# The last quarter of `w_down` in seven half-size products, with the sums leaving PSUM through ScalarE and adding transfers

## The chip, the core and the metric

The kernel runs on one core of one Trainium2 chip. The metric is the device time of one execution in microseconds (us). Before the change it is 1189.9 us, the median of three runs (1189.68 to 1191.11).

In what follows PE is the matrix engine (TensorE), DVE is VectorE, ACT is ScalarE, POOL is GpSimd and SP is the engine that issues most transfers (DMAs). SBUF is the on-chip memory that all of them work on, PSUM the small one that PE writes its sums to.

## What is computed

A trunk of two layers over 512 frames of 1024 features. Each layer is a mixer (two attention groups of eight heads, whose outputs meet in one projection) and a squared-ReLU MLP, each behind an RMS norm and added onto the residual stream. A last norm closes the trunk. The change is in the MLP, and in the first steps of both layers.

```python
def squared_relu_mlp(h, w_up, w_down):
    return jnp.square(jax.nn.relu(h @ w_up)) @ w_down

def reference(x, positions, norm_mix, norm_mlp, norm_final, w_in_ab, ...):
    for layer in range(DEPTH):                      # DEPTH = 2
        h = rmsnorm(x, norm_mix[layer])
        if layer % 2 == 0:
            x = x + even_mixer(h, w_in_ab[e], b_forget[e], rel_bias[e], w_out_ab[e])
        else:
            x = x + odd_mixer(h, positions, w_in_cd[o], ...)
        x = x + squared_relu_mlp(rmsnorm(x, norm_mlp[layer]), w_up[layer], w_down[layer])
    return rmsnorm(x, norm_final)
```

`w_up` is 1024 x 4096 and `w_down` 4096 x 1024 per layer. All of it is float32.

## The kernel before

**Numbers.** A float32 operand is split into a high part (rounded to the format that PE takes at full rate) and a low part, the difference. A product is three matmuls: high by high, high by low, low by high (`mm3`). ACT makes each high part (a cast), DVE each low part (a subtraction). The residual stream is four tiles `X[0]` to `X[3]`, each of 128 frames by 1024 features.

**Order.** Nothing is issued while the program is written. Every operation is recorded with a priority, and `Plan` then sorts all of them into one order per engine, by its own costs for each operation and by the rotation of the buffers. That order is fixed in the program: an engine that waits for one operation holds back everything behind it in its own queue. Almost all instructions carry the line of `Plan.issue` (L230), so groups are told apart by the names of their tiles.

**MLP.** The hidden layer's 32 chunks of 128 rows are four groups of eight. `up_pair` makes two chunks with 48 matmuls of 512 columns into the PSUM tiles `mm`; DVE applies the ReLU and the norm's factor (`ex`), ACT squares (`sq`). For groups 0 to 2, `seven_products` multiplies the group's 512 x 1024 activations by the 1024 x 1024 piece of `w_down`: both are cut into 2 x 2 blocks, and with sums and differences of blocks (`into`, on DVE) seven block products do the work of eight (Winograd's form of Strassen's scheme). One block product has 24 matmuls of 512 columns into two PSUM banks. The banks `main` (tiles `pa`) run on from one product to the next, `second` and `third` (tiles `pb`) are two other pairs. After each product `add` adds its two banks onto a half of two tiles of X: 14 DVE instructions in a group. The squares are four tiles of two chunks by 512 frames, and the first product of a group waits for all four.

Numbered as the code writes them, the products are: 1 into `main`, to X's rows 0 and left half; 2 into `second`, rows 1, right; 3 and 4 into `main`, rows 1, left and right; 5 into `second`, rows 1, left; 6 into `third`, rows 0, left; 7 into `main`, rows 0, right. Rows 0 are the tiles X[0] and X[1], rows 1 are X[2] and X[3]. Between products stand the `up_pair` calls of the next group, two matmul tiles of `mm` each.

Group 3 is done plainly: `up_split` squares and splits the activations, and two `add_proj` calls multiply them by the last eight chunks of `w_down`, 4 tiles of frames x 2 halves x 8 chunks x 3 = 192 matmuls of 512 columns. The second of them (`last=True`) finishes X[0] and X[1] first and the right halves last.

**Buffers.** Weight pages (`wh`, `wl`) share eight buffers of 1024 floats per partition, the raw `w_up` blocks (`wr`) two, the raw `w_down` blocks (`rw`) nine, the pages of split activations (`sh`, `sl`) six under the name `hd`. The tiles `p3`, 128 x 512, are two.

**Start.** `load_x` loads the four tiles of X; between them `first_loads` fetches the norm's gain, copied to 128 partitions by the transfer (512 KB), and the identity, and `first_weights` three blocks of `w_in_ab`. `norm_T` normalizes each tile and turns it to feature-major form `hT`. Sixty small matmuls on zeros (`warm`) run ahead of it, twelve more (`keep_warm`) after the first tile.

**Layer 1's values** (`step`, kind "v") are two blocks of 256 columns, so 2 x 4 x 8 x 3 = 192 matmuls of 256 columns; their weights are loaded ahead of `add_proj` at the end of layer 0.

Of the kernel before, what the change touches and what calls it, by code (L numbers as in the profile page):

```python
# [17 lines left out]
P = 128  # L18
# [8 lines left out]
WARM2 = 12  # L27
# [357 lines left out]
def trunk(ctx, tc, x, positions, norm_mix, norm_mlp, norm_final, w_in_ab, b_forget, rel_bias,  # L385
# [57 lines left out]
    def load_w(view, parts=None, place="w", raw_place="w"):  # L443
# [3 lines left out]
        if raw_place == "hd":  # L447
            raw = hp.tile([P, 1024], F32, tag="hd", name=nm("wr"))
        else:
            raw = wp.tile([P, 1024], F32, tag="wr", name=nm("wr"), bufs=2)  # L450
        if place == "hd":
# [71 lines left out]
    def norm_rows(xt, g, n):  # L523

        junk = otile()
        ss = small(1)
        nc.scalar.activation(junk.bitcast(BF16)[:, :n], xt, AF.Square, accum_out=ss)
        r = rstd_of(ss, n)
        pieces = []
        for c in range(0, n, S):  # L530
            m = min(S, n - c)
            t = etile()
            nc.vector.scalar_tensor_tensor(t[:, :m], xt[:, c:c + m], r, g[:, c:c + m], ALU.mult, ALU.mult)
            pieces.append(t)
        return pieces
# [19 lines left out]

    def norm_T_(X, g_row, g=None, after=None):

        g = gain(g_row, D) if g is None else g
        hT = [(utile(), utile()) for _ in range(NC // 2)]
        for t in range(NT):  # L560
            for h, piece in enumerate(norm_rows(X[t], g, D)):
                to_feature_major(piece, 4, hT[2 * h:2 * h + 2], t)
            if t == 0 and after is not None:
                after(hT)
# [48 lines left out]
    def col_blocks(w, kc, col, n, places=None, raw_place="w"):  # L613
# [6 lines left out]
        for k, place in places:  # L620
            b = load_w(rows(w, c, c + k, col, col + n), place=place, raw_place=raw_place)
# [194 lines left out]
    def seven_products(X, R, wd, k0):  # L816
# [15 lines left out]
        a11, a21, a12, a22 = ([R[j + i][:, :, q:q + 256] for i in range(2)] for j in (0, 2) for q in (0, 256))  # L832
# [14 lines left out]
        def product(banks, A, B, first):  # L847

            for i in range(4):
                for q in range(2):  # L850
                    a = tuple(h[:, i, q * P:(q + 1) * P] for h in A)
                    b = tuple(h[:, i % 2] for h in B[i // 2])
                    mm3(banks[q], a, b, first and i == 0, i == 3, skip_group_check=not first)
# [19 lines left out]
        yield  # L873

# [11 lines left out]

        into(b11, b21, b11, SUB)
        product(second, acts(a22), weights(b11), False)
        add(second, 1, 0)
        yield  # L890

        third = side()
        product(third, acts(a12), weights(b21), True)
        add(third, 0, 0)
        yield

        into(a21, a12, a21, SUB)
        product(main, acts(a21), weights(b22), False)
        add(main, 0, 1)
        yield  # L900

    def mlp(X, g_row, wu, wd, ahead=None):
# [36 lines left out]
        def squares():  # L939
            return [up.tile([P, 2, S], F32, tag="u", name=nm("sq")) for _ in range(4)]  # L940
# [4 lines left out]
        for g in range(3):  # L945
            steps = seven_products(X, R, wd, 8 * g)
            nxt = squares() if g < 2 else None
            act = []
            for pr, n in enumerate((2, 2, 2, 1)):
# [9 lines left out]
        nxt = up_split(3584)  # L959
# [21 lines left out]
    def first_loads():  # L981
        g0.append(gain(norm_mix[0:1, :], D))
        nc.sync.dma_start(ident, consts[:, O_ID:O_ID + P])

    def first_weights():
        early[0] = {1: col_blocks(w_in_ab, NC, 1280, 264, raw_place="hd")}

    early = {}
    X = load_x(xr, between={0: first_loads, 1: first_weights})
    def keep_warm(hT):  # L990
        a = hT[0][0][:, 0, 0:P]
        for _ in range(WARM2):
            nc.tensor.matmul(warm[:, 0:P], lhsT=a, rhs=a, start=True, stop=True)

    hT = norm_T(X, None, g=g0[0], after=keep_warm)

    early[0][0] = col_blocks(w_in_ab, NC, 1024, 256)
# [120 lines left out]
    mlp(X, norm_mlp[0:1, :], w_up[0], w_down[0], ahead=first_of_layer_1)  # L1118


# [131 lines left out]
    def step(name):  # L1252
        nonlocal vw, cq, ck, cqT, ckT, KR, o, wq, wkv
        kind, i = name.rstrip("01234567"), int(name[-1]) if name[-1].isdigit() else None
        if kind == "v":
            first, last = early["v"]
            tail = col_blocks(w_in_cd[6 * P:], 2, 1280, 256, [(2, "rd")])
            vw, _ = v_proj(w_in_cd, 1024, hT, w={0: first, 1: lambda c: last(c) if c < 6 else tail(c - 6)})
# [70 lines left out]
    mlp(X, norm_mlp[1:2, :], w_up[1], w_down[1])  # L1329
# [47 lines left out]
```

## Time and profile before

| | us |
|---|---|
| median of three runs | 1189.9 |
| the profiled execution | 1191.89 |
| its span, first to last instruction | 1190.2 |
| PE busy in the span | 1168.5 |
| DVE busy | 864.6 |
| ACT busy | 596.4 |
| POOL busy | 168.1 |

The profiled execution took 2.0 us more than the median of the runs, and 1.7 us of its time lie outside the span. A group's row in the profile gives out<-in by the tiles' names, shapes, count, then busy time and mean ns of one, then the idle time of the engine just before and what ended it. Matmuls are pipelined, so the mean of one (389 ns for 512 columns) is longer than the step from one to the next; the chain of waits, which counts each microsecond once, shows the step.

The stages of the span: start and layer 0's projections and attention to about 250 us, layer 0's MLP to about 590, layer 1's mixer to about 857, its MLP to 1183, and the last norm.

### The profile page before, as it was taken

The numbers are of one execution on the slowest core, as the hardware profiler recorded it, in microseconds if no ns is written. First come the engines' busy times: TensorE is split into PE (matmuls) and PEld (weight loads), VectorE is DVE, ScalarE is ACT, GpSimd is POOL, SyncE is SP. The second block draws the span as 40 slices with busy tenths as digits, with TensorE's granted clock in tenths as the row PEclk, the third lists the DMA queues.
The fourth block names the chain that finished last, engine by engine and source line by source line (L and its number), as shares of the span: only waits on it lengthen the run. The fifth ranks groups of instructions, "written<-read, shape, count | busy, mean of one in ns | idle before, by whom it ended". The sixth has DMA issues, their size and how long they took to land.

```text
span 1190.2 us, 16361 instructions
## 1 busy us (share of the span) xinstructions
PE 1168.5 (98%) x5962; PEld 990.9 (83%) x5962; DVE 864.6 (73%) x1452; ACT 596.4 (50%) x1066; POOL 168.1 (14%) x303
## 2 busy tenths in 40 slices
PE   8999999999999999999999998999999999999997
PEld 8988888788888888887898987788888888888886
DVE  6547888685977877776755879778768778687645
ACT  5347777544443444444435756566644434344423
POOL 2216522100000000000003718022100000000000
PEclk9999999999999999999999999899999999999999
DMA  6533335443143241215332230782622413321221
GB/s 200 152 94 110 93 85 169 154 156 89 36 141 107 67 146 53 71 36 172 119 105 62 60 120 30 178 226 76 213 71 71 155 58 121 109 71 36 85 92 71
DMA packets 101088, 126.85 MB, mean 107 GB/s; under 512 B 5304, under 2 KB 71232, under 8 KB 101008
## 3 DMA queue, kind: packets, MB, share of 16 engines
q1 hardware_dynamic: 100768, 125.50, 34.5%
q8 instruction: 47, 0.77, 0.2%
q0 software_dynamic: 240, 0.31, 0.2%
q14 instruction: 33, 0.27, 0.1%
HBM read 112.12 MB, written 4.23 MB: 98 GB/s over the span
## 4 chain that ended last, share of the span: by engine, by line
PE 89%; DVE 4%; DMA 4%; ACT 1%; issue 1%; POOL 0%; SPq 0%; POOLq 0%; ACTq 0%; DVEq 0%
PE mm L230 60%; PE pa L230 11%; PE pb L230 8%; PE tr L230 4%; PE sc L230 3%; PE av L230 3%; DMA KH<-KH 1%; DVE u L230 1%; DVE wl L230 1%; DMA X<-in_x_dram 1%; DVE ex L230 1%; DVE k L230 1%; ACT wh L230 1%; DMA wr<-in_w_down_dram 1%; DMA wr<-in_w_in_cd_dram 0%
## 5 line engine op out<-in xcount | busy, mean ns | idle before, releaser
L230 PE MATMUL mm<-u,wh 128*128 128x512 f32 (+1 forms) x1524 | 466.6, 384 | 1.1 <-DVE u L230 1.0
L230 PEld LDWEIGHTS mm<-u,wh 128*128 128x128 f32 x1524 | 281.1, 189 | 53.0 <-DVE u L230 1.8
L230 PE MATMUL mm<-u,wl 128*128 128x512 f32 (+1 forms) x762 | 292.5, 384 | 0.0
L230 PE MATMUL mm<-wh,u 128*128 128x512 f32 (+4 forms) x1008 | 269.6, 349 | 1.3 <-DVE o L230 0.6
L230 DVE TENSOR_TENSOR wl<-wr,wh 128x1024 fp32r<-128x1024 f32 (+5 forms) x152 | 173.8, 1149 | 74.5 <-ACT wh L230 73.7
L230 ACT CAST wh<-wr 128x1024 fp32r<-128x1024 f32 (+5 forms) x152 | 149.6, 988 | 152.3 <-PE mm L230 73.5
L230 PEld LDWEIGHTS mm<-wh,u 128*128 128x128 f32 x1008 | 176.1, 190 | 21.4 <-DVE X L230 1.2
L230 PE MATMUL mm<-wl,u 128*128 128x512 f32 (+4 forms) x504 | 175.1, 348 | 0.9 <-DVE wl L230 0.8
L230 PEld LDWEIGHTS mm<-u,wl 128*128 128x128 f32 x762 | 143.8, 189 | 26.0 <-DVE wl L230 0.2
L230 ACT CAST wh<-rw 128x1024 fp32r<-128x1024 f32 x84 | 88.5, 1054 | 114.3 <-PE mm L230 54.0
L230 DVE TENSOR_TENSOR wl<-rw,wh 128x1024 fp32r<-128x1024 f32 x84 | 102.8, 1224 | 57.0 <-ACT wh L230 56.5
L230 PEld LDWEIGHTS mm<-wl,u 128*128 128x128 f32 x504 | 95.7, 190 | 10.4 <-DVE wl L230 1.4
L230 POOL TENSOR_TENSOR sm<-sm,mhalf 128x1 f32<-128x1 f32 x28 | 20.2, 721 | 458.3 <-DVE sm L230 458.3
L230 POOL TENSOR_SCALAR p<-p,sm 128x128 f32<-128x128 f32 (+1 forms) x96 | 53.6, 558 | 175.7 <-DVE sm L230 129.9
L230 DVE TENSOR_TENSOR X<-mm,X 128x512 f32<-128x512 f32 x80 | 54.4, 687 | 28.8 <-PE mm L230 28.5
L230 PE MATMUL pa<-wl,sh 128*128 128x512 f32 x192 | 74.7, 389 | 0.0
L230 PE MATMUL pa<-wh,sl 128*128 128x512 f32 x192 | 74.7, 389 | 0.0
L230 ACT ACTIVATE sq<-ex 128x512 f32<-128x512 f32 x48 | 30.3, 631 | 88.5 <-DVE ex L230 88.5
L230 PE MATMUL pa<-wh,sh 128*128 128x512 f32 x192 | 74.4, 389 | 0.0
L230 DVE SCALAR_TENSOR_TENSOR ex<-mm,rstd 128x512 f32<-128x512 f32 x64 | 44.1, 688 | 39.5 <-PE mm L230 34.5
L230 PE MATMUL tr<-ident,p 128*128 128x128 f32 x320 | 65.6, 280 | 5.0 <-POOL p L230 3.5
L230 PE MATMUL av<-pt,u 128*128 128x128 f32 (+3 forms) x256 | 65.6, 340 | 0.0
(133 smaller groups left out, 1674.3 us busy)
## 6 DMA issues: line engine op xcount, KB each, us to landing
wr<-in_w_up_dram SPq DMA_DIRECT2D x64, 512.0 KB, 3.9
rw<-in_w_down_dram SPq DMA_DIRECT2D x48, 512.0 KB, 3.3
wr<-in_w_in_ab_dram SPq DMA_DIRECT2D x22, 512.0 KB, 3.9
wr<-in_w_down_dram SPq DMA_DIRECT2D x16, 512.0 KB, 3.3
wr<-in_w_in_cd_dram SPq DMA_DIRECT2D x11, 512.0 KB, 3.9
X<-in_x_dram SPq DMA_DIRECT2D x8, 512.0 KB, 6.3
wr<-in_w_out_ab_dram SPq DMA_DIRECT2D x8, 512.0 KB, 3.9
wr<-in_w_out_cd_dram SPq DMA_DIRECT2D x8, 512.0 KB, 3.9
```

Source lines behind the costliest of these rows:

```text
L230: getattr(getattr(self.nc, op.engine), op.method)(*op.args, **op.kw)
```

## The change

- `mlp` is called with `groups=4` in both layers: the last eight chunks go through `seven_products` as well, and `up_split`, the two `add_proj` calls and their splits are gone. In this last group (`last=True`) the products run in the order 1, 2, 6, 3, 4, 7, 5; product 6 takes `mm` banks; products 7 and 5 run one bank after the other (`apart`).
- `add` no longer uses DVE: ACT copies each bank into a tile `xa` (two buffers, tag `p3`), and a transfer issued by POOL adds it onto X in SBUF. Only products 5 and 7 of the last group still use DVE.
- The squares are laid out as the four blocks of the scheme, each 4 chunks by 256 frames, so product 1 needs only half the group's chunks. ACT writes each chunk in two instructions of 256 columns instead of one of 512, and the block sums and splits of activations are one instruction of 1024 columns instead of two of 512.
- Start: the gain comes as one row of 4 KB, and two matmuls with a row of ones spread it over PSUM. The first weights are loaded one block behind each tile of X. The two 512 KB blocks behind them wait until the first feature-major column exists. The twelve `keep_warm` matmuls are gone.
- Layer 1's values are one block of 512 columns: 96 matmuls of 512 columns instead of 192 of 256.

The core of the diff, with lines that only thread arguments left out:

```diff
-    def norm_T_(X, g_row, g=None, after=None):
+    def norm_T_(X, g_row, g=None):
...
-        a11, a21, a12, a22 = ([R[j + i][:, :, q:q + 256] for i in range(2)] for j in (0, 2) for q in (0, 256))
+        a11, a21, a12, a22 = ([r] for r in R)
...
+        def product(banks, A, B, first, apart=False):
+
+            for i, q in [(i, q) for q in range(2) for i in range(4)] if apart else [(i, q) for i in range(4) for q in range(2)]:
...
-        def add(banks, row, col):
+        def add(banks, row, col, final=False):
+
             for q in range(2):
                 xs = X[2 * row + q][:, col * S:(col + 1) * S]
-                nc.vector.tensor_tensor(xs, banks[q], xs, ALU.add)
+                if final or not (True):
+                    nc.vector.tensor_tensor(xs, banks[q], xs, ALU.add)
+                else:
+                    t = sp.tile([P, S], F32, tag="p3", name=nm("xa"))
+                    nc.scalar.copy(t, banks[q])
+                    nc.gpsimd.dma_start(xs, t, accum_op=ALU.add)
...
+        def second_row():
+
+            into(b11, b21, b11, SUB)
+            product(second, acts(a22), weights(b11), False, last)
+            add(second, 1, 0, last)
+
+        def first_row():
+
+            third = [mm_ps(), mm_ps()] if last else side()
+            product(third, acts(a12), weights(b21), True)
+            add(third, 0, 0)
+
+        if last:
+            first_row()
+            yield
...
+        into(a21, a12, a21, SUB)
+        product(main, acts(a21), weights(b22), False, last)
+        add(main, 0, 1, last)
         yield
...
+        if last:
+            second_row()
+            yield
...
             for m, r in enumerate(up_pair(1024 * g + 256 * pr, first=(g == 0 and pr == 0))):
-                nc.scalar.activation(R[pr][:, m], r, AF.Square)
+                for q in range(2):
+                    nc.scalar.activation(R[2 * (pr // 2) + q][:, 2 * (pr % 2) + m], r[:, 256 * q:256 * q + 256],
+                                         AF.Square)
...
-        for g in range(3):
-            steps = seven_products(X, R, wd, 8 * g)
-            nxt = squares() if g < 2 else None
+        for g in range(groups):
+            steps = seven_products(X, R, wd, 8 * g, last=g == 3)
+            if g == 3:
+
+                next(steps)
+                for pr in range(2, 4):
+                    up_raw(3, pr, R)
+                for _ in steps:
+                    pass
+                break
...
-        add_proj(X, act, 4, wd, 24)
-        add_proj(X, nxt, 4, wd, 28, last=True)
+        if groups == 3:
+            add_proj(X, act, 4, wd, 24)
+            add_proj(X, nxt, 4, wd, 28, last=True)
...
     def first_loads():
-        g0.append(gain(norm_mix[0:1, :], D))
+
+        row = utile(F32).rearrange("p a b -> p (a b)")
+        nc.sync.dma_start(row[0:1], norm_mix[0:1, :])
         nc.sync.dma_start(ident, consts[:, O_ID:O_ID + P])
+        one = etile()
+        nc.vector.memset(one[0:1, 0:P], 1.0)
+        for c in range(2):
+            ps = ps_sc.tile([P, S], F32, tag="sc", name=nm("gn"))
+            with nc.urgent(BOOST):
+                nc.tensor.matmul(ps, lhsT=one[0:1, 0:P], rhs=row[0:1, c * S:c * S + S], start=True, stop=True)
+            g0.append(ps)
+        some_weights(0, 3)
...
-    early[0][0] = col_blocks(w_in_ab, NC, 1024, 256)
+    early[0][0] = col_blocks(w_in_ab, NC, 1024, 256, late=f32(hT[0][0][:, P:P + 1]))
...
-        early["v"] = [col_blocks(w_in_cd, NC, 1024, 256, [(4, "hd"), (4, "hd")]),
-                      col_blocks(w_in_cd, NC, 1280, 256, [(4, "hd"), (2, "rd")])]
+        early["v"] = col_blocks(w_in_cd, NC, 1024, 512, [(2, "hd"), (2, "hd"), (2, "hd"), (1, "rd"), (1, "rd")])
...
-    mlp(X, norm_mlp[1:2, :], w_up[1], w_down[1])
+    mlp(X, norm_mlp[1:2, :], w_up[1], w_down[1], groups=4)
```

The order of the instructions at three places follows. The first is the middle of the MLP in layer 1, where a group's first two products end. Before, on DVE (`rw` are raw blocks of `w_down` and their sums, `wl` low parts of weights, `sl` of activations, `pa` and `pb` the banks):

```order
L230 TENSOR_TENSOR rw_2130<-rw_2132,rw_2128 128x1024
L230 TENSOR_TENSOR wl_2153<-wr_2151,wh_2152 128x1024
L230 TENSOR_TENSOR X_1647<-pa_2135,X_1647 128x512
L230 TENSOR_TENSOR X_1648<-pa_2136,X_1648 128x512
L230 TENSOR_TENSOR wl_2156<-wr_2154,wh_2155 128x1024
L230 TENSOR_TENSOR sl_2162<-sq_2024,sh_2161 128x512
```

Now, on ACT, at the same two products of the following group:

```order
L229 CAST sh_2346<-sq_2201 128x1024
L229 COPY xa_2334<-pa_2326 128x512
L229 CAST wh_2350<-rw_2319 128x1024
L229 COPY xa_2335<-pa_2327 128x512
L229 CAST sh_2364<-sq_2200 128x1024
L229 CAST wh_2355<-wr_2354 128x1024
L229 COPY xa_2344<-pb_2336 128x512
L229 CAST wh_2358<-wr_2357 128x1024
L229 COPY xa_2345<-pb_2337 128x512
```

The two additions have left DVE; on ACT a copy of a bank now stands between two casts of weights, and the copy of product 2's first bank (`xa_2344`) takes the buffer that product 1's (`xa_2334`) leaves when its transfer has landed.

The second place is the start of SP's queue. Before:

```order
L230 DMA X_101<-in_x_dram 128x1024
L230 DMA gain_102<-in_norm_mix_dram 128x1024
L230 DMA ident<-in_consts_dram 128x128
L230 DMA X_103<-in_x_dram 128x1024
L230 DMA wr_104<-in_w_in_ab_dram 128x3x264
L230 DMA wr_107<-in_w_in_ab_dram 128x3x264
L230 DMA wr_110<-in_w_in_ab_dram 128x2x264
L230 DMA X_113<-in_x_dram 128x1024
L230 DMA X_114<-in_x_dram 128x1024
```

Now:

```order
L229 DMA X_101<-in_x_dram 128x1024
L229 DMA u_102<-in_norm_mix_dram 1x1024
L229 DMA ident<-in_consts_dram 128x128
L229 DMA wr_106<-in_w_in_ab_dram 128x3x264
L229 DMA X_109<-in_x_dram 128x1024
L229 DMA wr_110<-in_w_in_ab_dram 128x3x264
L229 DMA X_113<-in_x_dram 128x1024
L229 DMA wr_114<-in_w_in_ab_dram 128x2x264
L229 DMA X_117<-in_x_dram 128x1024
```

The 512 KB of the gain are out of the way, and the weights that stood together ahead of X's third and fourth tile are spread between the tiles.

The third place is the end of ACT's queue, the last norm of X[2] and X[3] (`o` takes the squares of a half, `sm` their sum, `u` the output). Before:

```order
L230 ACTIVATE o_2381,sm_2382<-X_1649 128x512
L230 ACTIVATE o_2381,sm_2383<-X_1649 128x512
L230 ACTIVATE o_2387,sm_2388<-X_1650 128x512
L230 ACTIVATE u_2380<-u_2380,sm_2385 128x512
L230 ACTIVATE o_2387,sm_2389<-X_1650 128x512
L230 ACTIVATE u_2386<-u_2386,sm_2391 128x512
```

Now:

```order
L229 ACTIVATE o_2508,sm_2510<-X_1712 128x512
L229 ACTIVATE o_2514,sm_2515<-X_1713 128x512
L229 ACTIVATE u_2507<-u_2507,sm_2512 128x512
L229 ACTIVATE o_2514,sm_2516<-X_1713 128x512
L229 ACTIVATE u_2513<-u_2513,sm_2518 128x512
```

The rows read alike, but in the old order the last tile's left half, the first of its two `o` rows, is finished early and only the right half arrives last; in the new one the left half arrives last, and both `o` rows stand behind it.

More of the change, by code (lines that the diff above doesn't have):

```diff
@@ L450, in load_w @@
             raw = wp.tile([P, 1024], F32, tag="wr", name=nm("wr"), bufs=2)
+        if late is not None:
+            mark(raw, late)
         if place == "hd":
@@ L620, in col_blocks @@
         for k, place in places:
-            b = load_w(rows(w, c, c + k, col, col + n), place=place, raw_place=raw_place)
+            b = load_w(rows(w, c, c + k, col, col + n), place=place, raw_place=raw_place, late=late)
             for i in range(k):
@@ L814, in parts_of, with seven_products @@
         return hi, lo
[L816 removed]
+    def seven_products(X, R, wd, k0, last=False):
         def block(c, half):
@@ L885, in seven_products, with mlp @@
         yield
-        into(b11, b21, b11, SUB)
-        product(second, acts(a22), weights(b11), False)
-        add(second, 1, 0)
-        yield
[L892 to L902, printed above, removed]
+        if not last:
+            second_row()
+            yield
+            first_row()
+            yield
+        into(a21, a12, a21, SUB)
+        product(main, acts(a21), weights(b22), False, last)
+        add(main, 0, 1, last)
+        yield
+        if last:
+            second_row()
+            yield
+    def mlp(X, g_row, wu, wd, ahead=None, groups=3):
         hT, rstd = gained_T(X, g_row)
@@ L939, in squares @@
         def squares():
-            return [up.tile([P, 2, S], F32, tag="u", name=nm("sq")) for _ in range(4)]
+            return [up.tile([P, 4, 256], F32, tag="u", name=nm("sq")) for _ in range(4)]
         R = squares()
@@ L944, in mlp @@
             up_raw(0, pr, R)
-        for g in range(3):
-            steps = seven_products(X, R, wd, 8 * g)
-            nxt = squares() if g < 2 else None
+        for g in range(groups):
[7 more added lines that the diff above has]
+                break
+            nxt = squares() if g + 1 < groups else None
             act = []
-            for pr, n in enumerate((2, 2, 2, 1)):
+            for pr, n in enumerate((3, 3) if g == 2 and groups == 4 else (2, 2, 2, 1)):
                 for _ in range(n):
@@ L981, in first_loads, with some_weights @@
     def first_loads():
-        g0.append(gain(norm_mix[0:1, :], D))
+        row = utile(F32).rearrange("p a b -> p (a b)")
+        nc.sync.dma_start(row[0:1], norm_mix[0:1, :])
         nc.sync.dma_start(ident, consts[:, O_ID:O_ID + P])
+        one = etile()
[6 more added lines that the diff above has]
+        some_weights(0, 3)
+    first_of = {}
+    def some_weights(c, k):
+        b = load_w(rows(w_in_ab, c, c + k, 1280, 1544), raw_place="hd")
+        for i in range(k):
+            first_of[c + i] = tuple(h[:, i] for h in b)
     def first_weights():
-        early[0] = {1: col_blocks(w_in_ab, NC, 1280, 264, raw_place="hd")}
+        some_weights(3, 3)
+        early[0] = {1: first_of.get}
     early = {}
[L989 to L995, printed above, removed]
-    early[0][0] = col_blocks(w_in_ab, NC, 1024, 256)
+    X = load_x(xr, between={0: first_loads, 1: first_weights, 2: lambda: some_weights(6, 2)})
+    hT = norm_T(X, None, g=g0)
+    early[0][0] = col_blocks(w_in_ab, NC, 1024, 256, late=f32(hT[0][0][:, P:P + 1]))
     vw, ftail = v_proj(w_in_ab, 1024, hT, extra=8, order=(1, 0), w=early[0])
@@ L1255, in step @@
         if kind == "v":
-            first, last = early["v"]
-            tail = col_blocks(w_in_cd[6 * P:], 2, 1280, 256, [(2, "rd")])
-            vw, _ = v_proj(w_in_cd, 1024, hT, w={0: first, 1: lambda c: last(c) if c < 6 else tail(c - 6)})
+            vw = []
+            for t in range(NT):
+                vw.append(utile().rearrange("p a b -> p (a b)").rearrange("p (a n) -> p a n", n=256))
+                v_store(vw[t], token_proj(early["v"], hT, t, NC, S), 4)
         elif kind == "q":
```

26 lines of the change are left out of this document (12 added, 14 removed).

## The prediction

> **What bounds the kernel now.** I read the page's totals and the chain of waits first, then the table of stages, then the chain inside the MLP.
>
> ```profile
> PE 1168.5 (98%) x5962; PEld 990.9 (83%) x5962; DVE 864.6 (73%) x1452; ACT 596.4 (50%) x1066; POOL 168.1 (14%) x303
> PE 89%; DVE 4%; DMA 4%; ACT 1%; issue 1%; POOL 0%; SPq 0%; POOLq 0%; ACTq 0%; DVEq 0%
> ```
>
> ```profile
> 391.00:472.00 81.00, 81.00 (x359) 67.08 (x358) 62.87 (x74) 34.59 (x45) 0.00 (x0) 1.00 0.32 98
> 1058.00:1114.00 56.00, 56.00 (x248) 46.39 (x248) 43.98 (x53) 27.56 (x35) 0.00 (x0) 1.00 0.13 38
> 1184.00:1191.00 7.00, 0.00 (x0) 0.00 (x0) 1.48 (x4) 1.32 (x3) 0.55 (x1) 0.70 0.39 150
> ```
>
> Columns of the second fence: length, then busy us and instructions of PE, PEld, DVE, ACT, POOL, the granted clock, the DMA share, GB/s. In one group of the MLP (391 to 472) PE is busy for all 81 us, DVE for 63, ACT for 35. So here only fewer matmuls shorten anything, and the additions on DVE cost nothing. Only the last 7 us have no matmul.
>
> ```profile
> 330.39 5.44 PE pa L230 x24
> 335.83 0.68 PE mm L230 x3
> 336.51 5.44 PE pa L230 x24
> 605.69 1.08 PE mm L230 x9
> 1117.83 65.29 PE mm L230 x288
> ```
>
> The chain (start, length) gives the price of a matmul: 5.44 / 24 = 0.227 us for 512 columns, 1.08 / 9 = 0.12 us for 256 columns in layer 1's values. The last row is the end of layer 1: 96 matmuls of a pair of `up_pair` calls and the 192 of `add_proj`, without a gap. The 0.68 us between products 3 and 4, which share their banks, is filled with three matmuls of the next `up_pair`.
>
> **The change, part by part.**
>
> *Fewer matmuls.* Seven products of 24 instead of 192: 24 fewer per layer, 48 in all, 48 x 0.227 = **-10.9 us**. The order has exactly this count, so "it does not do what it says" is out. Layer 1's values: 192 x 0.12 = 23.0 us become 96 x 0.227 = 21.8: **-1.3 us**.
>
> *The additions.* DVE loses 108 of its 116 in the MLPs, 0.69 us each, which bought nothing; ACT gains 104 copies and POOL 104 transfers of 256 KB.
>
> ```profile
> L230 DVE TENSOR_TENSOR X<-pa,X 128x512 f32<-128x512 f32 x48 | 32.4, 690 | 3.1 <-PE pa L230 3.1
> L230 ACT COPY rstd<-rs 128x512 f32<-128x512 f32 x2 | 1.2, 586 | 4.8 <-PE rs L230 4.8
> L230 ACT CAST wh<-rw 128x1024 fp32r<-128x1024 f32 x84 | 88.5, 1054 | 114.3 <-PE mm L230 54.0
> L230 DVE TENSOR_TENSOR wl<-rw,wh 128x1024 fp32r<-128x1024 f32 x84 | 102.8, 1224 | 57.0 <-ACT wh L230 56.5
> ```
>
> The nearest row for a copy, PSUM to SBUF at this shape, is 0.59 us: 14 x 0.59 = 8.3 us more per group on ACT. With the squares in halves (a few us) that makes some 46 of 81 us, still far from PE. What counts is the order in the queue. A group's weights are just in time, as the timeline shows at a product that starts at 1090.63:
>
> ```profile
> 1090.63 5.44 PE pa L230 x24
> 1090.44 1.05 ACT L230 CAST wh<-rw 128x1024 fp32r<-128x1024 f32 x1 [1.67 <-PE mm L230]
> 1091.53 1.23 DVE L230 TENSOR_TENSOR wl<-rw,wh 128x1024 fp32r<-128x1024 f32 x1 [0.17 <-ACT wh L230]
> ```
>
> Its second page is ready at 1092.76 and needed after half the product, at 1090.63 + 2.72 = 1093.35: 0.6 us of cover. Now the copy of the earlier product's first bank stands ahead of that cast. The bank is complete three matmuls (0.68 us) before the product ends; with 0.2 us to wake ACT the copy runs to 0.1 us behind the end, the cast to 1.2, the subtraction to 2.4, and the page is needed at 2.7. About 0.3 us of cover stays, so I take 0, as long as the copy finds its buffer free. There are two buffers and two banks per product, so a copy waits for the transfer of the product before, 5.44 us earlier: a transfer must land within 5.44 - 0.59 = 4.85 us of its copy's end, 5.2 with the cover. No row shows an adding transfer. The nearest:
>
> ```profile
> Qm<-u SPq DMA_DIRECT2D x8, 256.0 KB, 3.8
> KH<-KH SPq DMA_DIRECT2D x24, 128.0 KB, 2.6
> posi<-in_positions_dram POOLq DMA_DIRECT2D x1, 256.0 KB, 5.3
> cd<-ex POOLq DMA_DIRECT2D x1, 16.0 KB, 1.8
> X<-in_x_dram SPq DMA_DIRECT2D x8, 512.0 KB, 6.3
> ```
>
> Bounds are 1.8 (POOL's queue, little data) and 6.3 (twice the data, beside other loads). I take about 4, next to the 256 KB from SBUF to SBUF (3.8) and under the 5.3 of POOL's load from HBM: inside 5.2, so **0**. The DMA engines stand at 0.32 of their share in the group, and 14 x 256 KB is 3.7 MB beside 98 GB/s x 81 us = 7.9 MB, so bandwidth is not short.
>
> For the same landing the Trainium skill (DMA: Bandwidth & Descriptors, Anatomy of one DMA — SWDGE (gpsimd) path) states 2.0 us plus bytes over 436 GB/s for a plain transfer from this queue; an estimate by that page is 2.6 us, and the term would be 0 as well.
>
> *The last group's order.* Products 3 and 4 now follow without a filler, so PE waits for ACT's copy: 0.2 + 0.59 + 0.1 - 0.68 = 0.2 us. In layer 1 a square of the last norm (0.63 + 0.19 us, rows below) stands ahead of that copy, and it waits for product 6's transfer. For both layers **+1.2**, bounds 0.4 and 5 (landing at 6.3 instead of 4, twice). Behind the last ReLU DVE has 17 instructions of 1.22 us (20.7 us) for products 6, 3, 4, 7 and 5, which take PE 27 us, so it is no bound.
>
> *Between the layers.* Today PE has no gap here:
>
> ```profile
> 588.00:590.00 2.00, 2.00 (x12) 1.63 (x11) 1.56 (x4) 1.41 (x3) 0.36 (x1) 1.00 0.51 209
> L230 ACT ACTIVATE o<-X 128x1024 bf16<-128x1024 f32 (+1 forms) x24 | 22.0, 918 | 32.1 <-DVE X L230 25.1 <-DMA X<-in_x_dram 7.0
> ```
>
> X[0] and X[1] used to be final 13.6 and 10.9 us before the MLP's last matmul (five and four `add_proj` parts of 2.72). Now product 7 finishes them 8.2 and 5.4 us before it, and X[2] 2.7. In ACT's order three squares of whole tiles (1.25 us each with the read-out) and two weight casts stand before the first cast of the new `hT`, and the third square waits for X[2] and its addition: 2.7 - 0.9 - 1.25 = 0.5 us before the last matmul, if DVE is free. The last weight pages of the values also need the `hd` buffers that product 5 holds to the end, then 1.05 + 1.22 us, against 2.7 us of matmuls that can go first. **+2**, bounds 0 and 4.
>
> *The start.*
>
> ```profile
> 12.00:13.00 1.00, 0.48 (x2) 0.32 (x3) 1.00 (x3) 0.00 (x0) 0.00 (x0) 0.79 1.00 404
> 13.00:14.00 1.00, 1.00 (x6) 1.00 (x6) 1.00 (x2) 0.76 (x1) 0.00 (x0) 0.50 1.03 382
> 16.00:17.00 1.00, 1.00 (x10) 1.00 (x10) 1.00 (x4) 1.00 (x3) 0.00 (x0) 1.00 0.32 95
> 18.71 1.83 PE mm L230 x13
> ```
>
> The DMA engines are full until 16 us. Ahead of X[2] stand 772 KB less, 2 us at 380 GB/s. From 18.71 the chain is PE's; before, PE waits, and for 3 us it runs at half its clock, 6 rows per us instead of 10. But DVE needs about 3 us per tile for the norm and the low parts, its order gets the first late weights before the fourth tile's low parts, and they now load late, so I take the 2 us of the data: **-2**, bounds -5 (all waits before 18.71 gone) and +1.5 (the slow stretch comes again, 3 us at half rate, and nothing is gained).
>
> On that stretch the Trainium skill (TensorE: Matmul & The Clock Gate, Part 1: The HAM clock gate) states that an idle window of about 3.4 us halves the clock; the rows agree, 0.50 after a thin stretch. With the twelve extra matmuls gone, the rule points to the upper bound, a total 3.5 us later.
>
> *The end.*
>
> ```profile
> 1183.15 0.69 DVE X L230
> 1183.88 0.63 ACT L230 ACTIVATE o<-X 128x512 bf16<-128x512 f32 x1 [0.42 <-DVE X L230]
> 1184.41 0.19 ACT L230 ACTIVATION_READ_ACCUMULATOR o<-X 128x1 f32 x1
> 1185.55 0.72 ACT L230 ACTIVATE u<-u,sm 128x512 f32<-128x512 f32 x1 [0.96 <-POOL sm L230]
> ```
>
> Behind the last addition stands one square now. In the new order the left half comes last, and behind its square (0.82) come another tile's scaling (0.72) and the right half's square: 0.72 + 0.82 = **+1.5**, bounds 0 and 2.
>
> *Sum:* -10.9 - 1.3 + 0 + 1.2 + 2 - 2 + 1.5 = -9.5 us on the profiled execution's 1191.89 us, 1182.4. That execution stands 2.0 us above the median of the runs, so the forecast is 1189.9 - 9.5 = **1180.4 us**, 0.8% faster. With all bounds at their ends the terms run from -16.8 to +0.3; the case's own range, its ends rarely meeting, is 1174 to 1187.
>
> **Rivals.**
>
> *A. The adding transfers land late, and ACT's queue stands (slower).* It decides from a landing of 5.2 us. Sites where the next copy follows within 5.44 us: products 2, 4, 6 in three groups and 6, 3, 4 in the last, 12 per layer, 24 in all; each us over costs up to 24 us. From 5.6 the gain is gone; at the 6.3 of X's loads it is 1.1 x 24 = 26 us, **1207**. For it: the transfer also reads what it adds to, POOL's one 256 KB transfer took 5.3, loads of 512 KB share the engines. Against: 3.8 and 2.6 from SBUF to SBUF.
>
> The Trainium skill (SBUF — State Buffer, SBUF: two separate sides) has a rule that speaks for A: while DVE runs an operation that uses both its ports, POOL cannot write its transfers' descriptors; it gives 0.62 us that become 3.1, and an estimate by that page puts a landing of 4 at 6.5. It names copies and scalar operations, and the MLP's DVE rows are two-input ones at single rate (1224 ns for 1024 elements), so by this trace the rule should not bite.
>
> *B. The ends eat the gain (no change).* Both seams fall out at their upper bounds (+4 and +5), the start gives nothing: -12.2 + 9 + 1.5 + 0 = -1.7, about **1188**. For it: X is final later, with fewer matmuls left to hide the norm. Against: the norm's chain has priority in the order.
>
> *C. The start gives all of its waits back and the seams cost little:* -12.2 - 5 + 0.4 + 0.5 + 1 = -15.3, **1174.6**. For it: the 3 us at half clock. Against: DVE's 3 us per tile.
>
> **How the numbers follow.** The forecast has 0.58, C 0.13, B 0.10, A 0.19. A measurement of this kernel can tell about 0.2% (2.4 us) from no change: faster is below 1187.5, slower above 1192.3. Faster: the forecast and C, and a little of B, 0.73; within 0.2%: the rest of B and the foot of A, 0.10; slower: the rest of A, 0.17. The range that holds 8 in 10 is 1174 to 1191; it leaves out most of A and the far side of C.
>
> **What would show it.** Right: 48 fewer matmuls of 512 columns in the MLPs, both still without a gap on PE, `pa` and `pb` products still 5.44 us in the chain; a landing of `X<-xa` near 4 us; idle time of ACT `wh` put down to PE, not to DMA; PE's first gapless stretch about 2 us earlier; 8 to 9 us between the last matmul and the end instead of 7. Wrong: ACT `xa` waiting for a DMA, `pa` rows cut into pieces by waits for ACT or DVE, over 4 us of PE idle between the layers.

## The result, and the profile after

The changed kernel takes **1179.8 us** (median of 5 runs, 1178.6 to 1181.6) against 1189.9 before: a ratio of 0.9913, 95% interval 0.9901 to 0.9924. That is 10.1 us less; the forecast was 1180.4. Its profiled execution took 1179.82 us, with a span of 1178.1. Of the executions of the experiments below one, with copies and transfers in the last group only, took 5520.8 us and stands outside its ratio.

The page of the changed kernel, its totals and the shares of its chain of waits:

```profile
PE 1156.5 (98%) x5810; PEld 974.5 (83%) x5810; DVE 835.9 (71%) x1311; ACT 666.4 (57%) x1198; POOL 258.1 (22%) x407
PE 89%; DVE 4%; issue 2%; DMA 2%; POOL 1%; ACT 1%; SPq 0%; POOLq 0%; ACTq 0%; DVEq 0%
```

PE is still the bound. It has 12 us less to do, ACT 70 us more, POOL 90 us more, and little of that shows in the chain, where POOL goes from 0 to 1%.

Where the time went is read from a few matmuls that both programs have. The rows of the view of one tile give, behind the count, the shortest, median and longest ns, then the start of the first and of the last. First before, then the changed kernel:

```profile
L230 PE MATMUL mm<-u,wh x1524: 278/389/797, 64.9 to 1139.0; 128*128 128x512 f32 x175, 128*128 128x256 f32 x16
L230 PE MATMUL pa<-wh,sh x192: 389/389/389, 308.5 to 1117.0; 128*128 128x512 f32 x192
L230 PE MATMUL mm<-ident,u x4: 272/272/273, 692.9 to 695.5; 128*128 128x128 f32 x4
L230 PE MATMUL rs<-ident,ex x8: 270/272/328, 261.2 to 857.5; 128*128 128x128 f32 x8
1182.72 0.39 PE L230 MATMUL mm<-wh,u 128*128 128x512 f32 x1
```

```profile
L229 PE MATMUL mm<-u,wh x1524: 278/389/793, 64.0 to 1135.7; 128*128 128x512 f32 x175, 128*128 128x256 f32 x16
L229 PE MATMUL pa<-wh,sh x256: 389/389/501, 306.1 to 1163.5; 128*128 128x512 f32 x128
L229 PE MATMUL mm<-ident,u x4: 271/272/273, 684.0 to 686.6; 128*128 128x128 f32 x4
L229 PE MATMUL rs<-ident,ex x8: 270/273/329, 258.8 to 848.7; 128*128 128x128 f32 x8
1168.94 0.39 PE L229 MATMUL pb<-wh,sl 128*128 128x512 f32 x1
```

The first `mm<-u,wh` stands right behind layer 0's values ("the values' row" below), the first `pa` is the first product of layer 0's MLP, the first `mm<-ident,u` stands in layer 1 behind its values, the last `rs` closes the norm in front of layer 1's MLP, and the last row of each is PE's last matmul. The seam is the passage from layer 0's MLP to layer 1.

| stretch | before | after | difference | the prediction's terms |
|---|---|---|---|---|
| start to layer 0's values | 64.9 | 64.0 | -0.9 | -2 (start) |
| on to layer 0's MLP | 243.6 | 242.1 | -1.5 | 0 |
| MLP of layer 0, seam, values of layer 1 | 384.4 | 377.9 | -6.5 | -5.45 - 1.3 + 0.6 + 2 = -4.15 |
| attention of layer 1 | 164.6 | 164.7 | +0.1 | 0 |
| MLP of layer 1 (to the start of PE's last matmul) | 325.2 | 320.2 | -5.0 | -5.45 + 0.6 = -4.85 |
| from there to the end of the span | 7.5 | 9.2 | +1.7 | +1.5 |
| sum | 1190.2 | 1178.1 | -12.1 | -9.5 |

The profiled execution of before stood 2.0 us above its median, so the 10.1 us between the medians, not these 12.1, are the result; the table tells where, to 1 or 2 us.

The stretches that answer to those of the prediction (length, then busy us and instructions of PE, PEld, DVE, ACT, POOL, granted clock, DMA share, GB/s): a group of the MLP, layer 0's last group, and the tail.

```profile
390.00:470.00 80.00, 80.00 (x355) 66.24 (x354) 52.37 (x48) 41.44 (x57) 12.06 (x14) 1.00 0.59 152
555.00:590.00 35.00, 34.96 (x158) 28.61 (x156) 33.29 (x38) 24.35 (x33) 8.00 (x10) 1.00 0.50 110
1169.40:1178.10 8.70, 0.00 (x0) 0.00 (x0) 3.11 (x7) 2.78 (x6) 1.53 (x2) 0.61 0.47 182
```

In the group PE still has no gap. ACT goes to 41 of 80 us, DVE falls to 52, and the DMA share rises from 0.32 to 0.59. In the last group DVE is busy for 33 of 35 us although only two of its products are still added by it.

The adding transfers, from the DMA issues and from the view of the tile `xa` (its landings, and what ACT's copies waited for in us and times):

```profile
X<-xa POOLq DMA_DIRECT2D x104, 256.0 KB, 4.5
DMA to landing us min/median/max: 3.2/4.5/7.9
PE pb L229: 19.3, 17
DMA X<-xa: 18.1, 22
```

Landings of 4.5 us in the median, inside the 5.2 us of the prediction, but with a long side: 22 copies had to wait for a buffer, 18.1 us in all. PE lost 0.28 us by it, once, at 509.83.

### The profile page after: what moved, and what is told of

The parts are those of the page before. It is cut to its first block, busy times and chain, and to the rows that moved or that the text cites. A ratio compares the mean times of both kernels' runs of the same rounds, so it can differ in the third digit from the quotient of the medians.

```text
span 1178.1 us, 16350 instructions
## 1 busy us (share of the span) xinstructions
PE 1156.5 (98%) x5810; PEld 974.5 (83%) x5810; DVE 835.9 (71%) x1311; ACT 666.4 (57%) x1198; POOL 258.1 (22%) x407
## 4 chain that ended last, share of the span: by engine, by line
PE 89%; DVE 4%; issue 2%; DMA 2%; POOL 1%; ACT 1%; SPq 0%; POOLq 0%; ACTq 0%; DVEq 0%
PE mm L229 55%; PE pa L229 14%; PE pb L229 10%; PE tr L229 4%; PE sc L229 3%; PE av L229 3%; DVE k L229 1%; DMA wr<-in_w_in_ab_dram 1%; DVE u L229 1%; DVE ex L229 1%; POOL p L229 1%; DVE wl L229 1%; DVE pt L229 0%; DMA X<-xa 0%; DMA KH<-KH 0%
## 5 line engine op out<-in xcount | busy, mean ns | idle before, releaser
L229 POOL DMA_DIRECT2D X<-xa x104 | 89.8, 867 | 527.2 <-ACT xa L229 527.1
L229 DVE TENSOR_TENSOR wl<-rw,wh 128x1024 fp32r<-128x1024 f32 x112 | 136.8, 1222 | 90.2 <-ACT wh L229 89.8
L229 PE MATMUL mm<-wh,u 128*128 128x512 f32 (+4 forms) x704 | 188.4, 347 | 1.6 <-DVE X L229 0.7
L229 ACT CAST wh<-rw 128x1024 fp32r<-128x1024 f32 x112 | 118.0, 1054 | 84.7 <-PE mm L229 62.7
L229 PEld LDWEIGHTS mm<-wh,u 128*128 128x128 f32 x704 | 121.9, 190 | 14.3 <-DVE X L229 1.3
L229 PE MATMUL mm<-wl,u 128*128 128x512 f32 (+4 forms) x352 | 121.0, 345 | 0.4 <-DVE wl L229 0.4
L229 ACT ACTIVATE sq<-ex 128x256 f32<-128x256 f32 x128 | 46.4, 409 | 108.2 <-DVE ex L229 108.2
L229 DVE TENSOR_TENSOR rw<-rw,rw 128x1024 f32<-128x1024 f32 x64 | 78.0, 1221 | 10.9 <-DMA rw<-in_w_down_dram 10.1
L229 DVE TENSOR_TENSOR sl<-sq,sh 128x1024 fp32r<-128x1024 f32 x56 | 68.3, 1220 | 9.0 <-ACT sh L229 8.8
L229 PEld LDWEIGHTS mm<-wl,u 128*128 128x128 f32 x352 | 67.0, 190 | 5.4 <-DVE wl L229 0.6
```

The costliest lines, as they stand in the source:

```text
L229: getattr(getattr(self.nc, op.engine), op.method)(*op.args, **op.kw)
```

## The experiments

Ratios are against the kernel before, measured on the same chip at the same time. Each has an interval of about 0.0012 to each side, so a difference of two ratios is known to about 2 us, and the traces have to place what is smaller. One thousandth is 1.2 us.

**All additions on DVE.**

```diff
-                if final or not (True):
+                if final or not (False):
```

> Four groups, but all 112 additions are done by DVE as before; no copy and no transfer onto X. If the gain is the 48 matmuls and the additions are free wherever they stand (the prediction's reading), the time stays within 2 us of the changed kernel's 1179.8: 1178 to 1182. Rival: the last group needs ACT and the transfers, because DVE has there 17 pages and sums of 1.22 us and 14 additions of 0.69 us, 30.4 us, against 27 us of PE: 3 us per layer more, 1184 to 1187, with PE waiting for DVE's low parts in the last group.

Measured: 1183.7 us, ratio 0.9944 (0.9931 to 0.9956), some 3.7 us more than the changed kernel. Where, by PE's timeline (start, length, in brackets what it waited for):

```profile
575.27 0.47 PE L229 MATMUL pa<-wh,sh 128*128 128x512 f32 x1 [0.58 <-DVE X L229]
581.16 0.47 PE L229 MATMUL pa<-wh,sh 128*128 128x512 f32 x1 [0.20 <-DVE X L229]
592.61 0.66 PE L229 MATMUL tr<-ident,ex 128*128 128x128 f32 x4 [0.32 <-DVE sm L229]
594.45 0.50 PE L229 MATMUL mm<-wh,u 128*128 128x512 f32 x1 [1.18 <-ACT u L229]
1156.61 0.47 PE L229 MATMUL pa<-wh,sh 128*128 128x512 f32 x1 [0.58 <-DVE X L229]
1162.50 0.47 PE L229 MATMUL pa<-wh,sh 128*128 128x512 f32 x1 [0.20 <-DVE X L229]
```

Both last groups lose 0.8 us to additions. Behind the seam it is 1.5 us more; the chain of waits goes there from ACT's casts over a weight load (588.84 to 593.00) and ACT's squares back to an addition on DVE at 585.1. The tail behind the last matmul is 0.9 us longer. The first three groups lose nothing. The rival holds, if at two thirds of its size, and with PE waiting for the additions themselves, not for DVE's low parts as it said. Free on DVE were the additions of the three groups, not those of the last one, which before stood under matmuls that needed little of DVE.

**Copies and transfers in the last group only.**

```diff
-                if final or not (True):
+                if final or not last:
```

> DVE makes the additions of the first three groups of each layer, as before; copies and transfers stay only in the last group (10 of 14 additions). With all additions on DVE the trace has PE waiting for DVE's additions only inside the last group (0.58 and 0.20 us in each layer) and behind it (1.5 us at the layer boundary, 0.9 us more in the tail). If that is the whole use of the copies: no change from the changed kernel, 0.991 of before, 1179.5 to 1181.5 us. Rival: the 84 transfers of the other groups also buy something (low parts that come earlier): 0.993 to 0.994, as with all additions on DVE.

Measured: 1179.4 us, ratio 0.9908 (0.9893 to 0.9923): the changed kernel's time. 84 of the 104 copies and transfers buy nothing; the 20 of the last groups are worth the 3.7 us. Their landing is 3.2 us in the median, as it was in layer 0's last group of the changed kernel, and no copy waits for a buffer any more.

**Three groups again.**

```diff
-    mlp(X, norm_mlp[0:1, :], w_up[0], w_down[0], ahead=first_of_layer_1, groups=4)
+    mlp(X, norm_mlp[0:1, :], w_up[0], w_down[0], ahead=first_of_layer_1, groups=3)
-    mlp(X, norm_mlp[1:2, :], w_up[1], w_down[1], groups=4)
+    mlp(X, norm_mlp[1:2, :], w_up[1], w_down[1], groups=3)
```

> The changed kernel with three groups of seven products and eight rows of matmuls at the end, as before; copies, transfers, start and values stay changed. If the gain is the matmuls: 48 x 0.227 = 10.9 us come back, the two 0.3 us waits of the last group and the longer tail (8.8 instead of 7.1 us) go: 1179.8 + 10.9 - 0.6 - 1.7 = 1188.4 us, 1187 to 1190. Rival: the start, the values and the freed DVE carry a good part of the gain: under 1185.

Measured: 1190.7 us, ratio 1.0000 (0.9991 to 1.0009), the time of before. So the fourth groups are worth about 10.4 us, more than the 8.6 expected, and no gain of the rest of the change can be told without them. Its trace shows one reason: PE waits in the third group of layer 0, for a cast that stands in ACT's queue.

```profile
552.81 0.50 PE L229 MATMUL mm<-wh,u 128*128 128x512 f32 x1 [1.34 <-ACT wh L229]
554.07 0.50 PE L229 MATMUL mm<-wl,u 128*128 128x512 f32 x1 [0.76 <-DVE wl L229]
```

The second of these waits is in the kernel before too (0.76 us at 556.06); only the first, 1.3 us, is new. By the terms, -2.3 for the start (below), -1.3 for the values and +1.3 us give -2.3 against before, and 0.0 with 1.1 to each side was measured. The spans of the two profiled executions, 1188.1 and 1190.2, differ by those 2 us, but the medians do not show it, and why is open.

**The fourth group in layer 0 only.**

```diff
-    mlp(X, norm_mlp[1:2, :], w_up[1], w_down[1], groups=4)
+    mlp(X, norm_mlp[1:2, :], w_up[1], w_down[1], groups=3)
```

> Layer 1 goes back to three groups, layer 0 keeps four. By the prediction's terms layer 1 gives back 24 x 0.227 = 5.4 us, less 0.3 us of wait in its last group and 1.7 us of tail: 3.4 us slower, 1183.3. Three groups in both layers cost 10.0 us, so layer 0 would be worth 6.6: more than its 5.4 us of matmuls. Rival: the layers share the 10.0 evenly (the tail is not what layer 1's fourth group costs): 1184.8.

Measured: 1183.5 us, ratio 0.9940 (0.9926 to 0.9953), 3.2 us more than the changed kernel. The sum for layer 1 gave 3.4 (5.4 - 0.3 - 1.7), the rival of equal shares 5.0; the times, known to about 2 us, allow both, and the rows decide. First this kernel's, then that of three groups in both layers:

```profile
L229 PE MATMUL rs<-ident,ex x8: 271/273/330, 258.9 to 848.7; 128*128 128x128 f32 x8
L229 PE MATMUL mm<-ident,u x4: 272/272/273, 691.2 to 693.8; 128*128 128x128 f32 x4
```

From 848.7 to the end of the span (1181.4) it is 332.7 us, where the changed kernel has 329.4: layer 1's fourth group is worth 3.3 us. With three groups in both layers the stretch of layer 0's MLP (306.5 to 691.2) is 384.7 us instead of 377.9: layer 0's is worth 6.8, 5.4 of matmuls and the 2.1 us of waits above, less what its last group and the seam cost.

**The old start.**

```diff
-    X = load_x(xr, between={0: first_loads, 1: first_weights, 2: lambda: some_weights(6, 2)})
-    hT = norm_T(X, None, g=g0)
-    early[0][0] = col_blocks(w_in_ab, NC, 1024, 256, late=f32(hT[0][0][:, P:P + 1]))
+    X = load_x(xr, between={0: first_loads, 1: first_weights})
+    hT = norm_T(X, None, g=g0[0], after=keep_warm)
+    early[0][0] = col_blocks(w_in_ab, NC, 1024, 256)
...
```

> The changed kernel with the start of before (broadcast gain, one load for the eight weight blocks, twelve matmuls behind the first transposed tile, no late loads). By PE's rows at 64 us the new start is 0.9 us ahead, at 306 us it is 2.4 us ahead; between them before waited 1.4 us for the transfer onto KH. If that wait comes from the start: 1179.8 + 2.4 = 1182.2. If it is scatter of one execution: 1179.8 + 0.9 = 1180.7. The prediction's 2.0 us would be 1181.8, with PE's row of the values at 64 us two us later.

Measured: 1182.5 us, ratio 0.9932 (0.9919 to 0.9946), about 2.3 us more. Its rows of the same two matmuls:

```profile
L230 PE MATMUL mm<-u,wh x1524: 278/389/797, 65.1 to 1138.3; 128*128 128x512 f32 x175, 128*128 128x256 f32 x16
L230 PE MATMUL pa<-wh,sh x256: 389/389/499, 308.3 to 1166.1; 128*128 128x512 f32 x128
209.91 0.33 PE L230 MATMUL sc<-KH,Q 128*128 128x128 f32 x1 [0.80 <-DMA KH<-KH]
```

Again 1.1 us at the values and 2.2 us at the MLP, most of the rest with a wait for the transfer onto `KH`. Before has it too (1.39 us at 210.07), and so has the longer warm-up below (1.71 us), which has the new loads; the eleven other profiled executions have none at that place. The order of PE's work around it is the same with both starts. The transfer took 7.5 to 8.5 us in those three and 6.2 to 6.7 in the others. Why is open, so the start is worth 1 us by its rows at the values and 2 by the times.

**No late loads.**

```diff
-    early[0][0] = col_blocks(w_in_ab, NC, 1024, 256, late=f32(hT[0][0][:, P:P + 1]))
+    early[0][0] = col_blocks(w_in_ab, NC, 1024, 256)
```

> The changed kernel without the mark that holds the two 512 KB weight blocks back. In the changed kernel they are issued at 19.5 us, land at 23.3, and PE waits for their low part until 25.73; the DMA engines are idle from 14 to 20 us. If this is what eats a part of the start's 2 us: PE's values begin (row at 64.0 us) 0.5 to 1.5 us earlier, 1178.3 to 1179.3. Rival: the blocks then share the DMA engines with the third and fourth tile of X, whose norm comes later: no change or up to 1 us slower.

Measured: 1181.8 us, ratio 0.9925 (0.9913 to 0.9938), 1.4 us more, which the times alone would not show; the values' row stands at 65.1. The rival fits: the DMA engines are then full until 16 us, ACT's square of the fourth tile of X starts at 17.60 instead of 17.07, and PE waits 1.3 us from 25.3 us on, now for DVE's addition `fl`. Two stretches of this kernel, and that wait:

```profile
14.00:16.00 2.00, 2.00 (x13) 2.00 (x12) 1.56 (x4) 1.04 (x1) 0.94 (x1) 0.58 1.05 388
24.00:26.00 2.00, 1.29 (x11) 1.08 (x9) 1.41 (x5) 1.58 (x5) 0.00 (x0) 1.00 0.00 0
PE mm L229 <- DVE fl L229: 1.3, 1, 1.3
```

**A longer warm-up.**

```diff
-WARM = 60
+WARM = 84
```

> 84 instead of 60 small matmuls at the start, so that PE is busy until about 10 us and does not stand idle from 7.8 to 10.4. Four executions with the same new start had a stretch at half clock of 0, 3.0, 3.4 and 7 us, and PE's row of the values stood at 64.2, 64.2, 64.0 and 65.4: a stretch up to 3.4 us cost nothing, because PE waited later (until 25.7 us) for the marked weight blocks. So the stretch goes and the time stays: 0 to -0.4 us on the mean, 1179.4 to 1179.9. Rival (the clock sets the start): the row at 62.5 to 63 and 1.5 us gained, 1178.3.

Measured: 1183.0 us, ratio 0.9931 (0.9919 to 0.9944), 2.1 us more: neither theory. In its profiled execution the small matmuls ran past 12 us, at half the rate that they have in the changed kernel's (35 in 3.91 us against 25 in 1.57). Three executions with sixty of them had that slow rate too (last section); there the first transposed tile came on PE at 11.28 and the values' row stood at 64.2, here at 12.35 and 65.1. The wait for `KH` adds 1.7. So it does not tell apart what it was made for, only that a granted clock of 1.00 throughout did not help a start that was 1 us later.

**The right half last.**

```diff
     for t in range(NT):
+        A, B = (slice(0, S), slice(S, D)) if t < 2 else (slice(S, D), slice(0, S))
         y = utile(F32).rearrange("p a b -> p (a b)")
```

> The changed kernel, with the halves of the last norm exchanged for the third and fourth tile of X, so that the half that is finished last is squared last. If the tail is long because two squares and a scaling stand behind the last addition (the prediction's term of 1.5 us): 8.8 us behind the last matmul become about 7.2, 1178.2 us. Rival: the tail waits for something else (the sums by DVE and POOL, the final transfers): no change, 1179.8.

Measured: 1178.6 us, ratio 0.9900 (0.9886 to 0.9913), 1.5 us less. Behind the last matmul:

```profile
1169.90:1177.10 7.20, 0.00 (x0) 0.00 (x0) 2.33 (x5) 2.07 (x5) 0.77 (x2) 0.63 0.52 201
```

7.2 us where the changed kernel has 8.7. The tail's term is shown by the rows; the two times alone, whose intervals overlap, would not show it.

**Both good edits.** The right half last, and copies and transfers in the last group only.

> The two edits that the runs point to together: copies and transfers only in the last group of each layer, and the halves of the last norm exchanged for two tiles. If they are independent: 0.9908 and 0.9900 against 0.9913 for the changed kernel, so 0.9895 of before, about 1178.0 us. Rival: the first edit is worth nothing by itself (its interval holds 0.9913), so 0.990, 1178.6.

Measured: 1178.2 us, ratio 0.9895 (0.9882 to 0.9909). It beats the kernel before by 1.0%; against the changed kernel it is 2 us down with intervals that just overlap, and from the right half alone it cannot be told.

**Layer 1's values as before.**

```diff
-        early["v"] = col_blocks(w_in_cd, NC, 1024, 512, [(2, "hd"), (2, "hd"), (2, "hd"), (1, "rd"), (1, "rd")])
+        early["v"] = [col_blocks(w_in_cd, NC, 1024, 256, [(4, "hd"), (4, "hd")]),
+                      col_blocks(w_in_cd, NC, 1280, 256, [(4, "hd"), (2, "rd")])]
...
```

> The changed kernel with layer 1's values as before: 192 matmuls of 256 columns and weight pages of four blocks. The prediction's term alone: 23.0 - 21.8 = 1.3 us slower, 1181.1. Rival: the pages of four blocks need two more buffers that the last products hold, so the first values wait at the seam, where the changed kernel has only 0.23 us: 3 to 5 us slower, 1183 to 1185.

Measured: 1185.4 us, ratio 0.9955 (0.9942 to 0.9967), 5.0 us more: the rival's size, though not for its reason. PE's timeline has eight waits behind the seam, 3.1 us in all, and none is for weights. Four of them, and below the only one that the changed kernel has there:

```profile
594.17 0.50 PE L229 MATMUL mm<-wh,u 128*128 128x256 f32 x2 [0.31 <-DVE u L229]
596.52 0.39 PE L229 MATMUL mm<-wh,u 128*128 128x256 f32 x1 [0.46 <-ACT u L229]
601.49 0.66 PE L229 MATMUL tr<-ident,ex 128*128 128x128 f32 x4 [0.84 <-DVE ex L229]
606.64 0.66 PE L229 MATMUL tr<-ident,ex 128*128 128x128 f32 x4 [0.44 <-DVE ex L229]
```

```profile
590.70 0.50 PE L229 MATMUL mm<-wh,u 128*128 128x512 f32 x1 [0.23 <-ACT u L229]
```

They are waits for the norm of the next tile of X; with the 1.3 us of columns they make 4.4 of the 5.0 us. With columns in one block of 512 each tile brings PE 24 x 0.227 = 5.4 us of work at once, with blocks of 256 only 24 x 0.12 = 2.9 us, so the norm has to come twice as fast. DVE is busy for 20 of the 22 us there.

**Each transfer twice.**

```diff
                     nc.gpsimd.dma_start(xs, t, accum_op=ALU.add)
+                    nc.gpsimd.dma_start(xs, t, accum_op=ALU.add)
```

> Each transfer onto X is issued twice (X gets each product twice: the output is not the reference's), so a buffer of a copy comes free later by a second issue and a second landing on the same queue, about 2 us by the gap from issue to issue. Rival A of the prediction (24 places where each us over 5.2 us of landing costs up to 1 us): landings of 6.5 in place of 4.5 give up to 24 x 1.3 = 31 us, 1211. Against it stands the changed kernel's trace: copies waited 18.1 us for buffers in 22 places, up to 2.3 us at once, and PE waited nowhere for that, because the copy that waits is the second of a pair and 96 matmuls of an up_pair follow. By that reading only the last group, where the products follow each other, pays: 4 places per layer, at most 1.3 us each, and the seam: 1180 to 1190.

Measured: 1223.8 us, ratio 1.0286 (1.0266 to 1.0306), 44 us more than the changed kernel. The second transfer adds onto the same rows of X and was held until the first had landed (POOL's second row below), so a buffer came free after two landings of 4.1 us, 8.2 us and more.

```profile
POOL X L229 <- ACT xa L229: 341.5, 100, 43.4
POOL X L229 <- DMA X<-xa: 150.8, 90, 5.7
ACT xa L229 <- DMA X<-xa: 134.5, 53, 7.3
PE pa L229 <- ACT xa L229: 11.4, 5, 4.8
PE pb L229 <- ACT xa L229: 5.1, 5, 1.5
```

ACT's 134 us of waits pass on to PE. Behind PE's pauses the granted clock was halved four times, 17 us in all (its mean from 510 to 520 us is 0.66); as an estimate, half of that, 8.5 us, is a part of the 44. My reading that only the last group would pay was wrong: it took the landing at 6.5 and left out the order onto X. Rival A's mechanism is real; by its price (8.2 - 5.2) x 24 = 72 us it is too dear by more than half.

**A transfer without adding.**

```diff
-                    nc.gpsimd.dma_start(xs, t, accum_op=ALU.add)
+                    nc.gpsimd.dma_start(xs, t)
```

> The transfers overwrite X instead of adding (the output is not the reference's). The landing of the adding transfer was 4.5 us (3.2 to 7.9). If reading the destination costs, as rival A argued: 3.3 us or less without it. If the landing is descriptors and shared engines: 4.2 to 4.5, and the copies' waits for buffers stay near 18 us.

Measured, in a single execution: 1180.3 us, beside before's 1190.7. The landing falls to 3.3 us, and ACT's waits for buffers from 18.1 to 2.0 us:

```profile
X<-xa POOLq DMA_DIRECT2D x104, 256.0 KB, 3.3
DMA X<-xa: 2.0, 1
```

So adding costs 1.2 us of landing, as rival A argued, and the 16 us of ACT's waits that go with it cost PE nothing: the time is that of the changed kernel.

## Why the prediction was right, point by point

The total came out 0.6 us from the forecast. Some of its terms were off by 1 to 3 us and cancelled, so that it is this close is luck; between the two profiled executions, which the sum started from, it was -12.1 us instead of -9.5.

**Fewer matmuls, -10.9 us:** right. The stretch of layer 1's MLP is 5.0 us shorter, for 5.4 less its waits; three groups in place of four cost 10.4 us.

**Additions at no cost on DVE ("which bought nothing"):** right for the three groups, wrong for the last. The step counted DVE's pages there (17 x 1.22 = 20.7 us against 27 of PE) only for the kernel whose additions are on ACT. With the additions on DVE it is the bound, and 20 of the 104 copies are worth 3.7 us.

**Landing, about 4 us and so 0:** the size was right (4.5), the time too, but not the point from which it decides. Copies waited 22 times, up to 2.30 us, where the prediction's 0.3 us of cover would have let PE stall. That `xa` waits for a DMA was one of its signs of being wrong, and it came without the cost. The changed kernel's ACT timeline shows the longest, and what follows it:

```profile
420.32 0.59 ACT L229 COPY xa<-pa 128x512 f32<-128x512 f32 x1 [1.03 <-PE pa L229]
424.15 0.59 ACT L229 COPY xa<-pa 128x512 f32<-128x512 f32 x1 [2.30 <-DMA X<-xa]
424.64 1.06 ACT L229 CAST sh<-sq 128x1024 fp32r<-128x1024 f32 x1
```

The waiting copy belongs to the last product before an `up_pair`, of which PE has 46 matmuls in hand meanwhile (10.43 us in the chain, from 420.92; an `up_pair` is 48, not the 96 of the expectation above); the casts for the next product can be late by about that. The cover was reckoned for two products in a row and then used for all 24 places. Two landings in series (8.2 us) go through it: 44 us.

The Trainium skill (DMA: Bandwidth & Descriptors, Anatomy of one DMA — SWDGE (gpsimd) path) gives 2.6 us for this size by the estimate in the prediction, farther off than the row of 3.8; plain transfers measured 3.3 here (2.2 to 6.0), adding ones 4.5. The rule of the Trainium skill on DVE and POOL's descriptors (SBUF — State Buffer, SBUF: two separate sides), which spoke for 6.5, did not bite: POOL's issue of an adding transfer took 0.85 to 1.07 us in all 104 cases. Nor was this a test of it, since DVE's rows here are the two-input ones that the prediction had set apart.

**The last group's order, +1.2:** about half. Product 4 starts 0.33 us late in each layer (0.43 us from the matmul before where the step is 0.227, and 0.34 to the next):

```profile
572.97 0.39 PE L229 MATMUL pa<-wh,sl 128*128 128x512 f32 x1
573.40 0.50 PE L229 MATMUL pa<-wh,sh 128*128 128x512 f32 x1
573.74 0.39 PE L229 MATMUL pa<-wl,sh 128*128 128x512 f32 x1
```

**Between the layers +2, and the values -1.3:** each mis-sized. The seam costs 0.23 us, because the 512-column values give PE twice the work per tile of X; the prediction priced that edit by PE's columns alone and the seam as if they had stayed. Undone, it costs 5.0 us, of which 3.1 are waits for the norm.

**The start, -2:** in its place by the times (2.3), less by the rows (0.9 at the values). The reason given, that the late loads hold it back, is half right. In all ten profiled executions with this start PE waits 0.3 to 0.4 us for the low part of the marked weights, between 25.7 and 27.6 us, and the values end 38.3 us behind that wait. But without the mark another wait takes its place and it is 1.4 us slower. What the mark waits for is a column of the second tile of X (the copy reads column 128, not the first one); ACT casts that tile from 15.97 on, while the copy that releases the loads stands at 19.36 in DVE's queue. An earlier place for it was not tried.

The stretch at half clock came again, as feared under the upper bound. The changed kernel:

```profile
8.00:10.00 2.00, 0.00 (x0) 0.00 (x0) 1.31 (x2) 1.40 (x2) 0.00 (x0) 1.00 1.06 395
10.00:12.00 2.00, 1.61 (x9) 1.38 (x10) 1.87 (x4) 1.79 (x5) 0.56 (x1) 0.70 1.06 409
12.00:14.00 2.00, 2.00 (x9) 1.75 (x9) 1.95 (x6) 1.80 (x5) 0.00 (x0) 0.50 0.75 297
```

It did not cost what that bound said. Of the ten executions three had no such stretch, and their values end at 64.2; five had one of 3.4 us, and theirs end at 64.0 to 64.7; only in the two with 6.8 us the marked loads go out later (at 20.9 and 21.4 instead of 19.5 to 20.1), and the values end at 65.4 and 65.9. So a stretch of 3.4 us is hidden by the later wait. The Trainium skill (TensorE: Matmul & The Clock Gate, Part 1: The HAM clock gate) has the clock halve after an idle window of about 3.4 us. Here it halved behind a pause of PE in all seven executions that have one, but the pauses were of 1.8 to 3.1 us.

**The end, +1.5:** right. 1.7 us by the rows, 1.5 given back with the halves exchanged.

**Rivals.** A did not happen, as the median landing stayed under the point, which lies higher than was said. B and C did not either: one seam cost 0.23 us and the tail 1.7, and the start gave 1 to 2 us.

## What to carry to other kernels

Work out an engine's load for the stretch in which the work will lie, not for the program: DVE had 18 us to spare in a group of 81 and none in the last one of 35, and only there did the additions have to move. A wait in a queue costs what stands behind it: 18 us of ACT's waits cost PE 0.28 us because an `up_pair` followed, and waits of twice that landing cost 44 us. And an edit that gives the engine that sets the end longer pieces of work per input gains more than its instructions say where those inputs are late: 1.3 us by its instructions, 5.0 in its place.

## What the hardware showed unexpectedly

- A transfer that adds costs more than a plain one on the same queue and at the same places: POOL is busy 867 ns instead of 540 for each issue, and the landing is 4.5 us instead of 3.3.
- Its landing also differs with the place: 4.6 to 5.0 us in the median in layer 0's first three groups, 3.2 for those issued from 555 to 595 us in its last, where the DMA engines move 110 GB/s instead of 152. That the load is the reason is not shown.
- The start differs between executions of the same start. In three of the ten the small matmuls on zeros ran at half the rate to their end (25 in 2.85 us instead of 1.57, with a granted clock of 1.00 on record in both), PE had no pause before the first transposed tile, and no stretch at half clock followed. In the other seven PE paused and the stretch came, 3.4 us long in five and twice that in two, as these rows of the kernel with all additions on DVE show, whose values ended at 65.4:

```profile
14.00:16.00 2.00, 2.00 (x11) 2.00 (x11) 1.14 (x3) 0.00 (x0) 0.95 (x1) 0.50 0.03 8
16.00:18.00 2.00, 2.00 (x12) 2.00 (x11) 0.34 (x1) 0.65 (x3) 0.00 (x0) 0.56 0.00 0
```
